# Query projection spread between the first attention steps, compressed-key softmax in two halves, six low parts on GpSimd

## The chip, the cores and the metric

The kernel runs on one core of a Trainium2 chip, in one launch. The metric is the device time of that launch in microseconds. Its engines are TensorE (PE; its weight loads are shown as PEld), VectorE (DVE), ScalarE (ACT), GpSimd (POOL) and the DMA queue of SyncE (SP). Each engine works through its own list of instructions in order and waits where an instruction needs what another engine has not yet delivered.

## The reference, cut to what matters

A two-layer decoder trunk for 256 tokens of width 1024, in float32: a retention layer with a dense SwiGLU, then a sparse-attention layer (16 heads in 4 groups) with a mixture of 8 experts. The change lies in the attention layer:

```python
proj = x @ w_q                                   # queries and gates
q = rotary(q, pos) * dh ** -0.5
gates = sigmoid(proj[..., H * dh:])              # three per head
sc = einsum('bgrqd,bgnd->bgrqn', qb, k_c)        # 15 compressed keys
p_cmp = masked_softmax(sc, cmp_end <= t)
o_cmp = einsum('bgrqn,bgnd->bgrqd', p_cmp, v_c)
...                                              # selected blocks, window
out = gb[..., 0:1] * o_cmp + gb[..., 1:2] * o_slc + gb[..., 2:3] * o_win
return out @ w_out
```

With 256 tokens every block is selected and the window holds all earlier tokens, so the second and the third branch are causal softmaxes over two sets of 256 keys (index `b` below).

## The kernel before

A list of steps is written out by hand (`step(units, fn)`), and the loop at the end of the program issues them in that order; the order of each engine's instructions follows from it. A unit is a piece of a weight matrix. It is loaded into a `raw` buffer by SP, and `convert` splits it into a high part (`whi`, a cast on ACT, L214) and a low part (`wlo`, the difference, on DVE, L215), so that a product takes three fast matmuls: high by high, low by high, high by low (L222 to L224). The loop converts up to `LOOK` = 3 units ahead of the step that uses them; a raw buffer is loaded again once both parts of its units are made. There are six `whi` and six `wlo` buffers.

The query projection has four groups `i` of 256 columns, with four units each (`b`, two of the eight rows of blocks of the contraction). `q_gemm(i, us, b)` does 12 matmuls for a unit, into two `acc` banks that are held until `b` = 3; then `rope` (four DVE instructions, L678 and L679, and two POOL additions, L684) makes `qn`, and `q_transpose(i)` turns it into two of the eight head pairs of `qT`.

Attention goes by head pairs `p` and token halves `t`. `att_scores(p, t)` multiplies queries and keys into two `mm` banks and adds the mask (L867, L870), takes the negative row maxima on DVE (L877, `anm`) and the exponentials with their sums on ACT (L879, `ae`, `asm`). `att_scale` turns the sums into weights (three small DVE instructions, L885 to L887) and scales the exponentials (L890, four instructions). `att_transpose` transposes them on PE and copies them out (`aPT`), and `att_values(p)` adds the compressed branch and the two others into one bank and splits it into `oh` and `ol`, a cast on ACT (L227) and a difference on DVE (L228).

`oh` and `ol` are made by `new_xT()` at `p` = 0. It allocates the same single pair of buffers, with the tags `xTh` and `xTl`, that holds the transposed input which the query projection reads.

The compressed branch has its own softmax for all 16 heads at once: `cmp_scores`, `cmp_weights`, `cmp_transpose`. After attention, `nsa_out` multiplies by the output weights (eight units of 128x1024, `nsa_o`), two layer norms follow, and the experts start. PSUM has four `mm` banks and four `acc` banks.

Of the kernel before, what the change touches and what calls it, by code (L numbers as in the profile page):

```python
# [10 lines left out]
F32 = mybir.dt.float32  # L11
F32R = mybir.dt.float32r
# [3 lines left out]
ALU = mybir.AluOpType  # L16
# [3 lines left out]
S = 256  # L20
NT = 2
# [5 lines left out]
NCMP = 15  # L27
# [57 lines left out]
class Unit:  # L85
    def __init__(self, raw, view, conv=True):
        self.raw = raw
        self.view = view
        self.conv = conv
        self.hi = self.lo = None  # L90
        self.own = False
        raw.left += 1


@with_exitstack
def tile_decoder(ctx, tc, x, ret_w_in, ret_gn_g, ret_w_out, nsa_w_kv, cmp_k_pe, cmp_k_w1, cmp_k_w2,
                 cmp_v_pe, cmp_v_w1, cmp_v_w2, nsa_w_q, nsa_w_out, ffn_w_in, ffn_w_out,
                 moe_router, moe_w_in, moe_w_out, ln_g, ln_b, tab_c, tab_r, out, wst, stop=None, cap=CAP):
    nc = tc.nc
# [8 lines left out]
    ident = sb.tile([128, 128], F32, name="ident")  # L108
# [96 lines left out]
    def convert(u, hi=None, lo=None):  # L205
        if not u.conv or u.hi is not None:
            return
        v = u.view(u.raw.ap)
        a, b = v.shape[1], v.shape[2]
        u.own = hi is not None  # L210
        u.hi = hi if u.own else side["pool"].tile([128, 1024], F32R, name="whi", tag="whi", bufs=NHL)
        u.lo = lo if u.own else side["pool"].tile([128, 1024], F32R, name="wlo", tag="wlo", bufs=NHL)
        u.hi, u.lo = (z[:, :a * b].rearrange("p (a b) -> p a b", a=a) for z in (u.hi, u.lo))
        nc.scalar.copy(u.hi, v)  # L214
        nc.vector.tensor_sub(u.lo, v, u.hi.bitcast(F32))  # L215
        release(u.raw)

    def step(units, fn, look=None):
        steps.append((units, fn, LOOK if look is None else look))
# [6 lines left out]
    def split(hi, lo, src):  # L226
        nc.scalar.copy(hi, src)  # L227
        nc.vector.tensor_sub(lo, src, hi.bitcast(F32))  # L228
# [135 lines left out]
    tsl = [slice(t * 128, (t + 1) * 128) for t in range(NT)]  # L364
# [4 lines left out]
    def open_phase(name):  # L369
        guard = tc.tile_pool(name=name, bufs=1, reuse_waits="tile")  # L370
        phases.append((guard, guard.__enter__()))
# [4 lines left out]
    def ptile(shape, dt, tag, bufs=1, lv=-1):  # L376
        return phases[lv][1].tile(shape, dt, name=tag, tag=tag, bufs=bufs)
# [285 lines left out]
    if stop not in ("r1", "r2"):  # L663
# [150 lines left out]
        def q_transpose(i):  # L814
            def f():
                ps = bank("acc")
                for t in range(NT):
                    for c in range(2):
                        nc.tensor.transpose(ps[:, c * 256 + t * 128:c * 256 + (t + 1) * 128],
                                            N["qn", i, t][:, 2 * c:2 * c + 2].rearrange("p h d -> p (h d)"), ident)  # L820
                nc.scalar.copy(N["qT"][:, 2 * i:2 * i + 2], ps.rearrange("p (c n) -> p c n", c=2))
            return f

        def cmp_scores():
            ps = bank("acc")
            for t in range(NT):
                for p in range(8):
                    nc.tensor.matmul(ps[:, (t * 8 + p) * 30:(t * 8 + p + 1) * 30], N["qT"][:, p, tsl[t]],
                                     N["kc"][:, p // 2].rearrange("p a n -> p (a n)"),
                                     start=t == 0 and p == 0, stop=True, skip_group_check=True)  # L830
            sc = ptile([128, NT, 16, NCMP], F32, "sc")
            shp = [128, NT, 16, NCMP]
            m = C[:, 264:294].rearrange("p (t n) -> p t n", t=2)[:, :, None, :].to_broadcast(shp)
            nc.vector.tensor_add(sc, ps[:, :480].rearrange("p (t h n) -> p t h n", t=2, h=16), m)
            mx = ptile([128, NT, 16], F32, "cmx")
            nc.vector.tensor_reduce(mx, sc, axis=AX.X, op=ALU.max)
            nc.vector.tensor_scalar(mx, mx, -1e29, None, op0=ALU.max)
            nc.vector.tensor_sub(sc, sc, mx[:, :, :, None].to_broadcast(shp))
            nc.scalar.activation(sc, sc, AF.Exp)
            N["ex"] = sc  # L840

        def cmp_weights():
            ex = N["ex"]
            sm = ptile([128, NT, 16], F32, "csm")
            nc.vector.tensor_reduce(sm, ex, axis=AX.X, op=ALU.add)
            nc.vector.tensor_scalar(sm, sm, 1e-30, None, op0=ALU.max)
            nc.vector.reciprocal(sm, sm)
            nc.vector.tensor_mul(sm, sm, N["gt"][:, :, :, 0])
            nc.vector.tensor_mul(ex, ex, sm[:, :, :, None].to_broadcast([128, NT, 16, NCMP]))

        def cmp_transpose():
            ps = bank("acc")
            for hb in range(2):
                for t in range(NT):
                    nc.tensor.transpose(ps[0:120, hb * 256 + t * 128:hb * 256 + (t + 1) * 128],
                                        N["ex"][:, t, hb * 8:hb * 8 + 8].rearrange("p h n -> p (h n)"), ident)
            hi, lo = ptile([120, 2, S], F32R, "pch"), ptile([120, 2, S], F32R, "pcl")
            split(hi, lo, ps[0:120].rearrange("p (b n) -> p b n", b=2))
            N["pcT"] = hi, lo

        def att_scores(p, t):

            g, n = p // 2, (t + 1) * 256
            ps = [bank() for _ in range(2)]
            for i in range(2):
                kt = N["kT"][i * 64:(i + 1) * 64, g].rearrange("p c b k -> p (c b k)")
                nc.tensor.matmul(ps[i][:, :n], N["qT"][i * 64:(i + 1) * 64, p, tsl[t]], kt[:, :n],  # L867
                                 start=True, stop=False, skip_group_check=True)
            for i in range(2):
                nc.tensor.matmul(ps[i][:, n - 256:n], identb, maskb.rearrange("p b k -> p (b k)"),  # L870
                                 start=False, stop=True, skip_group_check=True)
            e = ptile([128, 2, 2, t + 1, 128], F32, "ae%d" % t, bufs=2)
            sm = ptile([128, 2, 2], F32, "asm", bufs=6)
            nm = ptile([128, 2, 2], F32, "anm", bufs=6)
            for i in range(2):
                v = ps[i][:, :n].rearrange("p (c b k) -> p b c k", b=2, k=128)
                nc.vector.tensor_reduce(nm[:, i], v, axis=AX.XY, op=ALU.max, negate=True)  # L877
                for b in range(2):
                    nc.scalar.activation(e[:, i, b], v[:, b], AF.Exp, bias=nm[:, i, b:b + 1],  # L879
                                         accum_out=sm[:, i, b:b + 1])  # L880
            N["e", p, t] = e, sm

        def att_scale(p, t):
            e, sm = N["e", p, t]
            nc.vector.tensor_scalar(sm, sm, 1e-30, None, op0=ALU.max)  # L885
            nc.vector.reciprocal(sm, sm)
            nc.vector.tensor_mul(sm, sm, N["gt"][:, t, 2 * p:2 * p + 2, 1:3])  # L887
            for i in range(2):
                for b in range(2):
                    nc.vector.tensor_scalar(e[:, i, b], e[:, i, b], sm[:, i, b:b + 1], None, op0=ALU.mult)  # L890
# [88 lines left out]
        step([], lambda: kv_transpose(2))  # L979
        uqs = [units_q((wst['q0'], wst['q1']), i) for i in range(4)]  # L980

        def q_step(i):
            for b in range(4):
                step([uqs[i][b]], q_gemm(i, uqs[i], b))
                if i and b == 1:
                    step([], q_transpose(i - 1))

        q_step(0)
        step([], compress_out)
        step([], close_phase)  # L990
        step([], lambda: open_phase("nsa2"))
        for i in range(1, 4):
            q_step(i)
        step([], lambda: att_scores(0, 0))
        step([], lambda: att_scores(0, 1))
        step([], q_transpose(3))
        step([], lambda: att_scale(0, 0))
        step([], lambda: att_scale(0, 1))
        un = units_o(wst['nsa_o'], 0, 8)
        for p in range(7):  # L1000
            step([], lambda p=p: att_scores(p + 1, 0))
            step([], lambda p=p: att_transpose(p, 0))
            if p == 0:
                step([], cmp_scores)
            if p == 1:
                step([], cmp_transpose)
            step([], lambda p=p: att_scores(p + 1, 1))
            step([], lambda p=p: att_transpose(p, 1))
            step([], lambda p=p: att_scale(p + 1, 0))
            if p == 0:  # L1010
                step([], cmp_weights)
            else:
                step([], lambda p=p: att_values(p - 1))
            step([], lambda p=p: att_scale(p + 1, 1))
        nsa_out([0], un[0:1])
# [573 lines left out]
```

## Time and profile before

| what | value |
|---|---|
| time, median of 3 runs | 1461.58 us (1460.39 to 1463.45) |
| the profiled execution: its own time, and its span | 1460.46 us, 1458.7 us |
| PE matmul busy | 1355.4 us (93% of the span) |
| DVE, ACT, POOL busy | 471.3, 347.0, 62.7 us |
| query projection and attention, output projection | about 455 to 569 us of the span |
| experts | from about 589 us on |

The span runs from the first to the last instruction; the program's own time is 1.8 us longer. Busy shares are averages over stages with different limits, so the stage of the change is read by itself, from the timelines of single engines.

### The profile page before, as it was taken

Reading aid. Unit: us, or ns where it says so; the run is one execution under the profiler, and the core shown is the slowest. Engines: PE = TensorE matmul, PEld = TensorE weight load, DVE = VectorE, ACT = ScalarE, POOL = GpSimd, SP = SyncE. Lnnn points to the kernel's source line nnn. Section 1 sums busy time; section 2 is a strip of 40 time slices with the busy share of each in tenths; the row PEclk is TensorE's granted clock in tenths of the full one; section 3 lists DMA queues with packets and bytes.
Section 4 is the critical chain, followed back from the end, with each engine's and each line's share of the span. In section 5 each row is a group of like instructions: output and inputs, shape, how many; then the busy total and the mean of one; then the engine's idle time right before and its main releaser. Section 6 shows DMA issues by size and latency. Waiting matters only on the chain. (4 is left out here: it accounts for less than half of the span.)

```text
span 1458.7 us, 25366 instructions
## 1 busy us (share of the span) xinstructions
PE 1355.4 (93%) x11073; PEld 755.2 (52%) x11073; DVE 471.3 (32%) x845; ACT 347.0 (24%) x653; POOL 62.7 (4%) x74
## 2 busy tenths in 40 slices
PE   8999999999999988998999988888999988889995
PEld 7888888999978657432334332232333342222341
DVE  5755875554674886100100201001101101001002
ACT  4433434434534562200101110011001010000002
POOL 3101101000011000100000000000000000000000
PEclk9999999999999898999999999999999999999997
DMA  9736444544615308599999999999999999999970
GB/s 388 271 139 220 158 168 176 201 180 173 250 59 209 124 1 319 209 418 419 419 419 418 412 418 419 419 418 419 419 416 416 419 419 419 419 418 419 418 306 32
DMA packets 64022, 450.78 MB, mean 309 GB/s; under 512 B 7233, under 2 KB 7393, under 8 KB 10641
## 3 DMA queue, kind: packets, MB, share of 16 engines
q1 hardware_dynamic: 62208, 443.77, 75.4%
q0 software_dynamic: 1536, 4.98, 1.0%
q8 instruction: 106, 1.74, 0.5%
q14 instruction: 28, 0.22, 0.0%
q10 hardware_dynamic: 144, 0.07, 0.0%
HBM read 447.74 MB, written 1.05 MB: 308 GB/s over the span
## 5 line engine op out<-in xcount | busy, mean ns | idle before, releaser
L1202 PE MATMUL mm<-raw,xg 128*32 128x512 f32 (+1 forms) x2416 | 242.9, 544 | 11.5 <-DMA raw<-w_moe_a_dram 11.4
L1224 DVE TENSOR_TENSOR msh<-msh,mm 128x256 f32<-128x256 f32 (+1 forms) x96 | 35.5, 387 | 509.3 <-ACT msh L1223 509.3
L215 DVE TENSOR_TENSOR wlo<-raw,whi 128x1024 fp32r<-128x1024 f32 (+2 forms) x162 | 187.6, 1208 | 32.1 <-ACT whi L214 31.8
L1202 PE MATMUL mm<-ext,xg 128*32 128x512 f32 (+1 forms) x1808 | 178.8, 538 | 14.5 <-DMA ext<-w_moe_a_dram 14.5
L1202 PEld LDWEIGHTS mm<-raw,xg 128*32 128x32 f32 x2416 | 74.5, 110 | 164.4 <-issue 119.1
L214 ACT CAST whi<-raw 128x1024 fp32r<-128x1024 f32 (+2 forms) x162 | 153.7, 1008 | 18.6 <-PE acc L224 12.2
L1223 ACT ACTIVATE msh<-mm 128x256 f32<-128x256 f32 (+1 forms) x96 | 32.4, 357 | 492.9 <-PE mm L1202 492.9
L348 PE MATMUL mm<-xTh,whi 128*128 128x256 f32 x448 | 126.5, 282 | 1.6 <-ACT whi L214 1.6
L350 PE MATMUL mm<-xTh,wlo 128*128 128x256 f32 x448 | 125.9, 281 | 0.5 <-DVE wlo L215 0.5
L1261 PE MATMUL acc<-raw,hT 128*32 128x512 f32 x1000 | 116.5, 594 | 10.4 <-DMA raw<-w_moe_o_dram 9.2
L349 PE MATMUL mm<-xTl,whi 128*128 128x256 f32 x448 | 125.7, 281 | 0.0
L1202 PEld LDWEIGHTS mm<-ext,xg 128*32 128x32 f32 x1808 | 55.2, 110 | 129.3 <-issue 77.8
L1261 PE MATMUL acc<-ext,hT 128*32 128x512 f32 x864 | 98.4, 594 | 8.7 <-DMA ext<-w_moe_o_dram 8.7
L348 PEld LDWEIGHTS mm<-xTh,whi 128*128 128x128 f32 x448 | 84.7, 189 | 3.1 <-ACT whi L214 2.0
L350 PEld LDWEIGHTS mm<-xTh,wlo 128*128 128x128 f32 x448 | 84.7, 189 | 0.8 <-DVE wlo L215 0.8
L349 PEld LDWEIGHTS mm<-xTl,whi 128*128 128x128 f32 x448 | 84.7, 189 | 0.8
L1246 DVE COPY hT<-mm 128x256 f32<-128x256 f32 (+1 forms) x32 | 12.4, 389 | 223.2 <-PE mm L1239 223.2
L1261 PEld LDWEIGHTS acc<-raw,hT 128*32 128x32 f32 x1000 | 31.9, 110 | 87.9 <-issue 61.5
L1244 ACT COPY hT<-acc 128x512 f32<-128x512 f32 (+1 forms) x32 | 17.1, 536 | 230.6 <-PE acc L1239 150.1
L1202 PE MATMUL mm<-more,xg 128*32 128x512 f32 (+1 forms) x640 | 65.1, 535 | 4.9 <-DMA more<-w_moe_a_dram 4.8
L1261 PEld LDWEIGHTS acc<-ext,hT 128*32 128x32 f32 x864 | 26.4, 110 | 76.1 <-issue 50.8
L222 PE MATMUL mm<-whi,xTh 128*128 128x512 f32 (+1 forms) x144 | 55.6, 386 | 0.2 <-ACT xTh L227 0.2
(325 smaller groups left out, 1676.4 us busy)
## 6 DMA issues: line engine op xcount, KB each, us to landing
raw<-w_moe_a_dram SPq DMA_DIRECT2D x113, 1024.0 KB, 19.9
ext<-w_moe_a_dram SPq DMA_DIRECT2D x82, 1024.0 KB, 19.9
raw<-w_moe_o_dram SPq DMA_DIRECT2D x55, 1024.0 KB, 19.9
ext<-w_moe_o_dram SPq DMA_DIRECT2D x44, 1024.0 KB, 19.9
more<-w_moe_a_dram SPq DMA_DIRECT2D x29, 1024.0 KB, 19.9
raw<-w_ffn_b_dram SPq DMA_DIRECT2D x22, 1024.0 KB, 5.0
raw<-w_ret_a_dram SPq DMA_DIRECT2D x16, 1024.0 KB, 8.9
more<-w_moe_o_dram SPq DMA_DIRECT2D x13, 1024.0 KB, 19.9
```

The lines of the kernel that those rows point to most:

```text
L214: nc.scalar.copy(u.hi, v)
L215: nc.vector.tensor_sub(u.lo, v, u.hi.bitcast(F32))
L222: nc.tensor.matmul(ps, xh, wh, start=start, stop=False, skip_group_check=True)
L348: nc.tensor.matmul(ps, u.hi[:, k], xh[:, k], start=start and k == 0, stop=False, skip_group_check=True)
L349: nc.tensor.matmul(ps, u.hi[:, k], xl[:, k], start=False, stop=False, skip_group_check=True)
L350: nc.tensor.matmul(ps, u.lo[:, k], xh[:, k], start=False, stop=k == KD - 1, skip_group_check=True)
L1202: nc.tensor.matmul(M["A", g][j * 32:(j + 1) * 32, :n], M["xg", e // 2][:, k, e % 2, g * 32:(g + 1) * 32], v[:, kk, j], start=k == 0, stop= ...
L1223: nc.scalar.activation(sh[:, g, :w], M["A", g][:, :w], AF.Silu)
L1224: nc.vector.tensor_mul(sh[:, g, :w], sh[:, g, :w], M["A", g][:, w:2 * w])
L1244: nc.scalar.copy(dst, src)
L1246: nc.vector.tensor_copy(dst, src)
L1261: nc.tensor.matmul(M["y", g][q:q + 32], hT[0][:, g, cc, j * 32:(j + 1) * 32], v[:, c, h], start=s == 0 and i == 0, stop=s == 3 and i == 1, ...
```

## The change

The four units of the query groups 2 and 3 no longer come ahead of the attention steps but one by one behind `att_scores`: two in the opening (scores of pair 0), two in each of the turns `p` = 0, 1, 2. The compressed softmax is done for heads 0 to 7 at `p` = 0, 1 and for heads 8 to 15 at `p` = 3, 4. The sums of both token halves of a pair lie in one tile, and the three small instructions run once for a pair, in `att_scale(p, 0)`, instead of twice. The low parts of the first six output units are made by GpSimd instead of VectorE.

```diff
-        nc.vector.tensor_sub(u.lo, v, u.hi.bitcast(F32))
+        (nc.gpsimd if u.pool else nc.vector).tensor_sub(u.lo, v, u.hi.bitcast(F32))
...
-        def cmp_scores():
+        def cmp_scores(hb):
+
             ps = bank("acc")
             for t in range(NT):
-                for p in range(8):
-                    nc.tensor.matmul(ps[:, (t * 8 + p) * 30:(t * 8 + p + 1) * 30], N["qT"][:, p, tsl[t]],
+                for q in range(4):
+                    p = 4 * hb + q
+                    nc.tensor.matmul(ps[:, (t * 4 + q) * 30:(t * 4 + q + 1) * 30], N["qT"][:, p, tsl[t]],
                                      N["kc"][:, p // 2].rearrange("p a n -> p (a n)"),
...
-            sm = ptile([128, 2, 2], F32, "asm", bufs=6)
+            if t == 0:
+                N["asm", p] = ptile([128, NT, 2, 2], F32, "asm", bufs=4)
+            sm = N["asm", p][:, t]
...
-            nc.vector.tensor_scalar(sm, sm, 1e-30, None, op0=ALU.max)
-            nc.vector.reciprocal(sm, sm)
-            nc.vector.tensor_mul(sm, sm, N["gt"][:, t, 2 * p:2 * p + 2, 1:3])
+            if t == 0:
+                a = N["asm", p]
+                nc.vector.tensor_scalar(a, a, 1e-30, None, op0=ALU.max)
+                nc.vector.reciprocal(a, a)
+                nc.vector.tensor_mul(a, a, N["gt"][:, :, 2 * p:2 * p + 2, 1:3])
...
+        un = units_o(wst['nsa_o'], 0, 8)
+        for u in un[:6]:
+            u.pool = True
         step([], lambda: att_scores(0, 0))
+        q_unit(2, 0)
         step([], lambda: att_scores(0, 1))
+        q_unit(2, 1)
+        step([], q_transpose(1))
         step([], lambda: att_scale(0, 0))
         step([], lambda: att_scale(0, 1))
-        un = units_o(wst['nsa_o'], 0, 8)
+        more = {0: [(2, 2), (2, 3)], 1: [(3, 0), (3, 1)], 2: [(3, 2), (3, 3)]}
         for p in range(7):
             step([], lambda p=p: att_scores(p + 1, 0))
+            if p in more:
+                q_unit(*more[p][0])
             step([], lambda p=p: att_transpose(p, 0))
-            if p == 0:
-                step([], cmp_scores)
-            if p == 1:
-                step([], cmp_transpose)
+            if p in (0, 3):
+                step([], lambda p=p: cmp_scores(p // 3))
+            if p in (1, 4):
+                step([], lambda p=p: cmp_transpose(p // 3))
             step([], lambda p=p: att_scores(p + 1, 1))
+            if p in more:
+                q_unit(*more[p][1])
             step([], lambda p=p: att_transpose(p, 1))
+            if p in (1, 2):
+                step([], q_transpose(p + 1))
             step([], lambda p=p: att_scale(p + 1, 0))
-            if p == 0:
-                step([], cmp_weights)
-            else:
+            if p in (0, 3):
+                step([], lambda p=p: cmp_weights(p // 3))
+            if p:
                 step([], lambda p=p: att_values(p - 1))
```

In the changed kernel the lines named here are 1 to 17 higher: L215 is L216, L227 is L228, L877 is L881, L879 is L883, L684 is L685.

On VectorE, at the opening of attention, the maxima of the scores of pair 0 and of pair 1 stand close together before:

```order
L877 TENSOR_REDUCE anm<-mm 128x2 x4
L885 TENSOR_SCALAR asm<-asm 128x4
L886 RECIPROCAL asm<-asm 128x4
L887 TENSOR_TENSOR asm<-asm,gt 128x4
L890 TENSOR_SCALAR ae_4566<-ae_4566,asm 128x128 x4
```

In the changed kernel a low part of a query unit stands behind each pair of maxima:

```order
L881 TENSOR_REDUCE anm<-mm 128x2 x2
L216 TENSOR_TENSOR wlo<-raw,whi 128x512
L881 TENSOR_REDUCE anm<-mm 128x2 x2
L216 TENSOR_TENSOR wlo<-raw,whi 128x512
L891 TENSOR_SCALAR asm<-asm 128x8
L892 RECIPROCAL asm<-asm 128x8
L893 TENSOR_TENSOR asm<-asm,gt 128x8
L896 TENSOR_SCALAR ae_4390<-ae_4390,asm 128x128 x4
```

What moved: on ACT the high part (`whi`) of each such unit stands behind the exponentials of the same scores, and the low part here needs it.

On TensorE, around the first `att_values` (bank `acc_4697`) of the changed kernel, with buffer numbers (`xTh_3765` is the transposed input; `oh` is `xTh_4709` in the same memory):

```order
L933 MATMUL acc_4697<-aPT_4499,vn_3889 64x128 x2
L869 MATMUL mm_4717<-kT_3888,qT_4246 128x256
...
L223 MATMUL acc_4614<-whi_4536,xTh_3765 128x256
...
L906 MATMUL acc_4751<-ident_63,ae0_4599 128x128 x4
L869 MATMUL mm_4757<-kT_3888,qT_4246 128x512
...
L223 MATMUL acc_4614<-whi_4608,xTh_3765 128x256
L224 MATMUL acc_4614<-wlo_4609,xTh_3765 128x256
...
L820 MATMUL acc_4811<-ident_63,qn_4787 128x128 x2
```

What moved: the last two units of the projection, which read `xTh_3765`, now stand behind the first `att_values`, whose result is to be written to `xTh_4709`; before, all of them stood ahead of attention.

On GpSimd, the same stretch of the changed kernel (before, the eight `qn` additions followed each other with nothing but a memset between them):

```order
L685 TENSOR_TENSOR qn_4552<-t1k_4553,t1k_4554 128x256
L685 TENSOR_TENSOR qn_4558<-t1k_4559,t1k_4560 128x256
L216 TENSOR_TENSOR wlo_4657<-raw_4161,whi_4656 128x1024
L216 TENSOR_TENSOR wlo_4733<-raw_4161,whi_4732 128x1024
L216 TENSOR_TENSOR wlo_4772<-raw_4179,whi_4771 128x1024
L685 TENSOR_TENSOR qn_4787<-t1k_4788,t1k_4789 128x256
L685 TENSOR_TENSOR qn_4793<-t1k_4794,t1k_4795 128x256
```

What moved: three low parts of output units stand ahead of the additions that finish query group 3 (`qn_4787`, `qn_4793`), which PE's `q_transpose(3)` waits for.

## Rows read from the trace of the kernel before

**Rows 1.** Busy time by stretch: length, engines, granted clock, DMA share, GB/s.
```profile
468.65:544.85 76.20, 69.06 (x460) 47.35 (x459) 62.14 (x190) 45.73 (x165) 5.17 (x6) 0.93 0.22 83
...
498.00:506.00 8.00, 6.94 (x31) 4.61 (x33) 5.63 (x16) 3.69 (x15) 0.00 (x0) 0.57 0.00 0
...
544.85:569.04 24.19, 24.19 (x131) 19.14 (x130) 13.46 (x19) 7.25 (x10) 1.11 (x2) 1.00 0.68 261
...
589.00:603.00 14.00, 13.97 (x134) 4.12 (x126) 0.55 (x2) 2.25 (x5) 0.00 (x0) 1.00 0.01 2
...
700.00:1300.00 600.00, 552.49 (x5351) 195.02 (x5347) 64.08 (x144) 54.11 (x131) 5.94 (x12) 1.00 1.01 418
```
**Rows 2.** DVE timeline (start, length, instruction): opening and the turns' maxima.
```profile
470.71 2.01 DVE L215 TENSOR_TENSOR wlo<-raw,whi 128x512 fp32r<-128x512 f32 x2
...
483.98 1.94 DVE L877 TENSOR_REDUCE anm<-mm 128x2 f32<-128x256 f32 x4
...
489.46 0.75 DVE L877 TENSOR_REDUCE anm<-mm 128x2 f32<-128x256 f32 x2
...
500.50 0.75 DVE L877 TENSOR_REDUCE anm<-mm 128x2 f32<-128x256 f32 x2
...
509.50 1.94 DVE L877 TENSOR_REDUCE anm<-mm 128x2 f32<-128x256 f32 x4
...
516.61 1.94 DVE L877 TENSOR_REDUCE anm<-mm 128x2 f32<-128x256 f32 x4
```
**Rows 3.** ACT timeline: table load, exponentials, copies, casts.
```profile
479.29 2.00 ACT L214 CAST whi<-raw 128x1024 fp32r<-128x1024 f32 x2
481.31 1.28 ACT L879 ACT_TABLE_LOAD   x1
...
489.91 0.37 ACT L879 ACTIVATE ae<-mm,anm 128x128 f32<-128x128 f32 x1 [1.68 <-DVE anm L877]
...
491.30 0.60 ACT L901 COPY aPT<-acc 128x512 f32<-128x512 f32 x1
...
494.27 0.47 ACT L879 ACTIVATE ae<-mm,anm 128x256 f32<-128x256 f32 x1
...
496.09 0.60 ACT L912 COPY aPT<-acc 128x512 f32<-128x512 f32 x1
```
**Rows 4.** DVE timeline: low parts, compressed scores, one steady turn.
```profile
466.74 2.73 DVE L215 TENSOR_TENSOR wlo<-raw,whi 128x512 fp32r<-128x512 f32 x4
...
491.38 0.66 DVE L834 TENSOR_TENSOR sc<-acc,C 128x480 f32<-128x480 f32 x1 [1.17 <-PE acc L828]
...
512.55 0.87 DVE L890 TENSOR_SCALAR ae<-ae,asm 128x128 f32<-128x128 f32 x4
514.61 0.42 DVE L228 TENSOR_TENSOR xTl<-acc,xTh 128x256 fp32r<-128x256 f32 x1 [1.18 <-ACT xTh L227]
...
515.56 1.14 DVE L890 TENSOR_SCALAR ae<-ae,asm 128x256 f32<-128x256 f32 x4
```
**Rows 5.** PE timeline: two query units, then one steady turn.
```profile
478.52 0.37 PE L222 MATMUL acc<-whi,xTh 128*128 128x256 f32 x1
...
481.44 0.70 PE L867 MATMUL mm<-kT,qT 64*128 64x256 f32 x4
...
516.96 0.36 PE L222 MATMUL acc<-pch,vbh 120*128 120x256 f32 x1
...
518.94 0.70 PE L867 MATMUL mm<-kT,qT 64*128 64x256 f32 x4
...
520.86 1.20 PE L867 MATMUL mm<-kT,qT 64*128 64x512 f32 x4
```
**Rows 6.** POOL, timeline, then groups by form (busy us, mean ns, idle).
```profile
483.57 1.41 POOL L684 TENSOR_TENSOR qn<-t1k 128x256 f32<-128x256 f32 x2 [5.71 <-DVE t1k L679]
...
L408 POOL TENSOR_TENSOR rok<-t4k 128x256 f32<-128x256 f32 x4 | 6.9, 1716 | 0.0
...
L287 POOL TENSOR_TENSOR ygb<-msh,raw 128x512 f32<-128x512 f32 x2 | 2.5, 1268 | 183.1 <-ACT msh L286 183.1
```

More of the change, by code (lines that the diff above doesn't have):

```diff
@@ L91, in __init__ @@
         self.own = False
+        self.pool = False
         raw.left += 1
@@ L822, in q_transpose @@
             return f
-        def cmp_scores():
+        def cmp_scores(hb):
             ps = bank("acc")
             for t in range(NT):
-                for p in range(8):
-                    nc.tensor.matmul(ps[:, (t * 8 + p) * 30:(t * 8 + p + 1) * 30], N["qT"][:, p, tsl[t]],
+                for q in range(4):
+                    p = 4 * hb + q
+                    nc.tensor.matmul(ps[:, (t * 4 + q) * 30:(t * 4 + q + 1) * 30], N["qT"][:, p, tsl[t]],
                                      N["kc"][:, p // 2].rearrange("p a n -> p (a n)"),
-                                     start=t == 0 and p == 0, stop=True, skip_group_check=True)
-            sc = ptile([128, NT, 16, NCMP], F32, "sc")
-            shp = [128, NT, 16, NCMP]
+                                     start=t == 0 and q == 0, stop=True, skip_group_check=True)
+            shp = [128, NT, 8, NCMP]
+            sc = ptile(shp, F32, "sc", bufs=2)
             m = C[:, 264:294].rearrange("p (t n) -> p t n", t=2)[:, :, None, :].to_broadcast(shp)
-            nc.vector.tensor_add(sc, ps[:, :480].rearrange("p (t h n) -> p t h n", t=2, h=16), m)
-            mx = ptile([128, NT, 16], F32, "cmx")
+            nc.vector.tensor_add(sc, ps[:, :240].rearrange("p (t h n) -> p t h n", t=2, h=8), m)
+            mx = ptile([128, NT, 8], F32, "cmx", bufs=2)
             nc.vector.tensor_reduce(mx, sc, axis=AX.X, op=ALU.max)
@@ L839, in cmp_scores, with cmp_weights @@
             nc.scalar.activation(sc, sc, AF.Exp)
[L840 to L844, printed above, removed]
+            N["ex", hb] = sc
+        def cmp_weights(hb):
+            ex = N["ex", hb]
+            sm = ptile([128, NT, 8], F32, "csm", bufs=2)
             nc.vector.tensor_reduce(sm, ex, axis=AX.X, op=ALU.add)
@@ L847, in cmp_weights, with cmp_transpose @@
             nc.vector.reciprocal(sm, sm)
-            nc.vector.tensor_mul(sm, sm, N["gt"][:, :, :, 0])
-            nc.vector.tensor_mul(ex, ex, sm[:, :, :, None].to_broadcast([128, NT, 16, NCMP]))
-        def cmp_transpose():
+            nc.vector.tensor_mul(sm, sm, N["gt"][:, :, hb * 8:(hb + 1) * 8, 0])
+            nc.vector.tensor_mul(ex, ex, sm[:, :, :, None].to_broadcast([128, NT, 8, NCMP]))
+        def cmp_transpose(hb):
             ps = bank("acc")
[L853 to L859, printed above, removed]
+            for t in range(NT):
+                nc.tensor.transpose(ps[0:120, tsl[t]], N["ex", hb][:, t].rearrange("p h n -> p (h n)"), ident)
+            if hb == 0:
+                N["pcT"] = ptile([120, 2, S], F32R, "pch"), ptile([120, 2, S], F32R, "pcl")
+            hi, lo = N["pcT"]
+            split(hi[:, hb], lo[:, hb], ps[0:120, 0:256])
         def att_scores(p, t):
@@ L980, in tile_decoder, with q_unit @@
         uqs = [units_q((wst['q0'], wst['q1']), i) for i in range(4)]
-        def q_step(i):
+        def q_unit(i, b):
+            step([uqs[i][b]], q_gemm(i, uqs[i], b))
+        for i in range(2):
             for b in range(4):
-                step([uqs[i][b]], q_gemm(i, uqs[i], b))
+                q_unit(i, b)
                 if i and b == 1:
                     step([], q_transpose(i - 1))
[L988 to L993, printed above, removed]
+            if i == 0:
+                step([], compress_out)
+                step([], close_phase)
+                step([], lambda: open_phase("nsa2"))
+        un = units_o(wst['nsa_o'], 0, 8)
+        for u in un[:6]:
+            u.pool = True
         step([], lambda: att_scores(0, 0))
+        q_unit(2, 0)
         step([], lambda: att_scores(0, 1))
-        step([], q_transpose(3))
+        q_unit(2, 1)
+        step([], q_transpose(1))
         step([], lambda: att_scale(0, 0))
         step([], lambda: att_scale(0, 1))
-        un = units_o(wst['nsa_o'], 0, 8)
+        more = {0: [(2, 2), (2, 3)], 1: [(3, 0), (3, 1)], 2: [(3, 2), (3, 3)]}
         for p in range(7):
             step([], lambda p=p: att_scores(p + 1, 0))
+            if p in more:
+                q_unit(*more[p][0])
             step([], lambda p=p: att_transpose(p, 0))
-            if p == 0:
-                step([], cmp_scores)
-            if p == 1:
-                step([], cmp_transpose)
+            if p in (0, 3):
+                step([], lambda p=p: cmp_scores(p // 3))
+            if p in (1, 4):
+                step([], lambda p=p: cmp_transpose(p // 3))
             step([], lambda p=p: att_scores(p + 1, 1))
+            if p in more:
+                q_unit(*more[p][1])
             step([], lambda p=p: att_transpose(p, 1))
+            if p in (1, 2):
+                step([], q_transpose(p + 1))
             step([], lambda p=p: att_scale(p + 1, 0))
-            if p == 0:
-                step([], cmp_weights)
-            else:
+            if p in (0, 3):
+                step([], lambda p=p: cmp_weights(p // 3))
+            if p:
                 step([], lambda p=p: att_values(p - 1))
```

## The prediction

> **What bounds the kernel now.** Read the busy times by stretch first [rows 1]. From 700 to 1300 us the transfers run at 418 GB/s and a DMA share of 1.01, so the experts are paced by their weights. Just ahead of that, from 589 to 603 us, next to nothing is moved (2 GB/s): every buffer is full and SP waits until the first expert frees one. The whole rest therefore starts when attention and output projection are done, and a microsecond gained or lost there comes out one for one at the end. The output projection (544.85 to 569.04) has PE busy for 24.19 of 24.19 us, so what DVE and POOL do there lies under PE. Query group 2 to the end of attention, 468.65 to 544.85, takes 76.20 us with PE busy for 69.06 and DVE for 62.14: neither is full, the stretch is a chain between engines.
>
> The second view is DVE's timeline [rows 2]. Each turn of the attention loop begins with the row maxima. The rope of query group 1 ends at 470.71, where the next instruction starts; the first maxima come at 483.98, then 489.46, 500.50, 509.50 and 516.61, and from there a turn takes 7.1. So the first three turns take 5.5, 11.0 and 9.0 us; the second and third hold the whole compressed softmax, and part of them ran with PE at 1.2 GHz (0.57 of the clock granted from 498 to 506 [rows 1]).
>
> A turn is a chain DVE, ACT, DVE: maxima, exponentials of both halves on ACT, then on DVE the scaling, then the next maxima. The prices on it: 0.45 from the start of the maxima to the first exponential (489.46 to 489.91), 1.39 for the four exponentials of half 0 and 1.82 for those of half 1, 0.6 for a copy, 1.0 for a cast of 1024 columns, so about 0.5 for 512 [rows 3]. For half 1 I take 0.7 to the first exponential (an estimate, between 0.45 and twice that). On DVE: 0.68 for a low part of 512 columns (2.73 for four), 0.87 and 1.14 for the scalings, 0.95 from `xTl` to the end of the three small instructions, that is 0.35 and 0.6 [rows 4].
>
> **What the change takes away.** Eight query units leave the front of attention. In the new order the maxima of pair 0 stand right behind the group-1 rope, so they can start at 470.71 instead of 483.98: **13.3 us earlier**. Half of the small trios go (8 x 0.6 = 4.8 us of DVE), but the trio now also needs the exponentials of half 1. In a steady turn DVE today waits for the cast of `oh`, which stands on ACT behind those exponentials (1.18 [rows 4]); in the new order the trio and the first scaling wait there instead. I cost this at nothing; without that cover it is 0.6 a turn either way. The six low parts that leave DVE free nothing on the path, since PE is full in the output projection; if that cover were gone, each would cost some 1.2 more there (2 x 1.268 on POOL, as in the last group of rows, against at most 2 x 0.68).
>
> **What it adds, turn by turn.** A unit's high part stands on ACT behind the exponentials, its low part on DVE ahead of the next maxima or scaling, so all of it falls into the chain.
>
> Turn 0 to 1: 0.45, the table load 1.28 (hidden before, it ended at 482.59 while ACT still waited [rows 3]), 1.39, cast 0.5, low part 0.68, 0.7, 1.82, cast 0.5, low part 0.68, trio 0.6, scalings 0.87 and 1.14. Together 10.6 against 5.5: **+5.1**.
>
> Turn 1 to 2: the same without the table load (9.3), with half of the compressed maxima block and half of its weights (each about 1.3: three instructions of 240 columns near 0.37, estimated between 0.66 for 480 and 0.42 for 256 columns [rows 4], and small ones), the rope of group 2 (1.4, four of 256 columns) and a copy 0.6. Together 13.9 against 11.0: **+2.9**.
>
> Turn 2 to 3: 0.45, 1.39, cast 0.5, copy 0.6, the compressed cast and difference 0.7, 0.7, 1.82, cast of an output unit 1.0, copy 0.6: 7.8 until PE can start `att_values(0)`. Its result goes to `oh`, which lies in the memory of the transposed input, and the last readers of that are the units (3, 2) and (3, 3), behind it on PE. So ACT's cast waits for values 1.98 (516.96 to 518.94), scores and transposes of half 0 1.92 (to 520.86), a query unit 1.46 (two in 2.92, 478.52 to 481.44), scores of half 1 1.6 (1.20 and the masks), a second unit 1.46 [rows 5]: 8.4. Behind that cast on ACT stand all exponentials of pair 3; behind DVE's difference stands the scaling that PE's transposes need. With cast 0.4, difference 0.35 and scaling 1.14 the turn is 18.1 against 9.0: **+9.1**, 6.4 of it the wait for the old buffer.
>
> Turn 3 to 4: `q_transpose(3)` stands ahead of `att_values(1)` on PE and needs `qn` of group 3, which on POOL stands behind three low parts; the last of these needs the third output cast, behind the exponentials of pair 3. So: 0.45, 1.39, cast 1.0, copy 0.6, 1.82, cast 1.0, low part 2.5 (2 x 1.268), two additions 1.4 (1.41 for two) [rows 6], transposes 0.4, values 1.98, cast 0.4, difference 0.35, scaling 1.14. Together 14.4 against 7.1: **+7.3**.
>
> Turn 4 to 5 takes in the second half of the compressed maxima and weights, **+2.6**; turn 5 to 6 their cast and difference between the two exponentials, **+0.7**. The rest is as before.
>
> The turns grow by 27.7 and the start gains 13.3: **+14.4**. Two prices are open. PE idles for some 5 us in turn 3 to 4; if it falls to 1.2 GHz as from 498 to 506, values, scores and transposes behind that double: nothing to +4. A low part on POOL costs 2.5 from the 1268 ns row, but 6.9 at the `rok` row's 1716 ns for 256 columns; DVE mostly waits while the one that counts runs, so the lower row is the nearer. I take 1.5 for both: +15.9. On the profiled execution's 1460.46 us (span 1458.7 and 1.8 around it) that is 1476.4; the median of the runs is 1.1 above that execution, so **1477**.
>
> The Trainium skill (SBUF — State Buffer, Who interferes with whom) says that a VectorE instruction with two SBUF inputs and a GpSimd instruction that reads SBUF exclude each other, the second waiting for the whole first. The rows agree: 1716 ns for `rok`, which runs beside DVE's low parts, against 0.70 us for `qn` of the same size [rows 6]. By it a low part on POOL would wait for up to one DVE instruction, about 1.0 each, and the sum would be 1478 instead of 1477.
>
> **Rivals.** *PE fills its gaps (faster).* The units take PE's idle 7.1 us (76.20 less 69.06), DVE has 8.4 us less to do (the trios and three low parts of about 1.2 that lie in this stretch), and the stretch shrinks to PE's work: 1454. For it: DVE's 62.14 is far below the span. It decides when the turns grow by less than 13.3 instead of 27.7, that is, if neither long wait exists and the units cost about 1.5 each in the chain. Against it: both waits follow from the order of in-order engines. Chance 0.07.
>
> *The two effects cancel (no change).* The turns grow by about 13: 1459 to 1464, which needs one of the long waits gone and the first turns half as long. 0.05.
>
> *One long wait is mostly covered.* If ACT reaches the `oh` cast late, or POOL makes its low parts early, 4 to 10 us go: 1467 to 1473. For it: in a steady turn that cast stands 4 us behind the maxima anyway. 0.14.
>
> *POOL at the `rok` price.* One low part of 6.9 in turn 3 to 4 is +4.4, and the clock may add up to 4: 1480 to 1486. For it: `rok` is the same operation beside the same DVE work. 0.12.
>
> *The forecast,* 1472 to 1481: 0.62.
>
> **How the numbers follow.** About 0.2% (2.9 us) is what a measurement of this kernel can tell from no change. Slower by more than that are the forecast, the covered wait and the dear POOL: 0.88. Same 0.05, faster 0.07. The range 1465 to 1485 leaves out the first two rivals and a little of the last, under 0.2.
>
> **What would show it.** First maxima about 13 us earlier; the turns then some 10.6, 13.9, 18.1 and 14.4 us long; a wait of ACT at the first cast of `oh` of about 6 us, ended by a PE matmul of the query projection; a wait of PE at `q_transpose` for POOL's `qn` of several us; the table load between the first maxima and the first exponential; GpSimd low parts near 2.5; the expert stage as long as before. I am wrong if the turns stay near 7 to 11 us, which would mean that the high and low parts are made beside the exponentials and not between them, or if the expert stage changes its length.

## The result, and the profile of the changed kernel

The changed kernel takes 1481.93 us (median of 4 runs, 1481.40 to 1483.16) against 1462.16: ratio 1.0131, 95% interval [1.0109, 1.0153], 19.8 us slower. The forecast was 1477 us, and slower. Its profiled execution took 1482.43 us with a span of 1480.5. Ratios are compared below, not medians: executions of one kernel differ by up to 9 us with the stretches in which PE runs at half speed (in two profiles of the changed kernel its granted clock from 465 to 470 us was 1.00 and 0.75, and the first maxima came at 471.27 and 472.96; in that of `own_buffer` it was 0.50, and they came at 474.24).

DVE's timeline of the changed kernel, the maxima that begin a turn, answers to [rows 2]:

```profile
471.27 0.75 DVE L881 TENSOR_REDUCE anm<-mm 128x2 f32<-128x256 f32 x2
482.05 0.74 DVE L881 TENSOR_REDUCE anm<-mm 128x2 f32<-128x256 f32 x2
496.50 0.75 DVE L881 TENSOR_REDUCE anm<-mm 128x2 f32<-128x256 f32 x2
513.58 1.94 DVE L881 TENSOR_REDUCE anm<-mm 128x2 f32<-128x256 f32 x4
529.38 0.74 DVE L881 TENSOR_REDUCE anm<-mm 128x2 f32<-128x256 f32 x2
539.05 0.75 DVE L881 TENSOR_REDUCE anm<-mm 128x2 f32<-128x256 f32 x2
547.64 1.94 DVE L881 TENSOR_REDUCE anm<-mm 128x2 f32<-128x256 f32 x4
554.75 1.34 DVE L881 TENSOR_REDUCE anm<-mm 128x2 f32<-128x256 f32 x3
```

The first maxima come 12.7 us earlier (483.98 in [rows 2]). The turns then take 10.8, 14.5, 17.1, 15.8, 9.7, 8.6 and 7.1 us; before they took 5.5, 11.0, 9.0 and four times 7.1. That is 29.7 us more. From the timelines of single engines, the rows that make the two longest turns, and one behind them:

```profile
471.75 1.28 ACT L883 ACT_TABLE_LOAD   x1 [2.53 <-issue]
...
503.42 3.02 DVE L896 TENSOR_SCALAR ae<-ae,asm 128x128 f32<-128x128 f32 x4
...
511.79 0.37 ACT L228 CAST xTh<-acc 128x256 fp32r<-128x256 f32 x1 [7.13 <-PE acc L224]
512.19 0.42 DVE L229 TENSOR_TENSOR xTl<-acc,xTh 128x256 fp32r<-128x256 f32 x1 [5.75 <-ACT xTh L228]
...
518.64 1.09 ACT L215 CAST whi<-raw 128x1024 fp32r<-128x1024 f32 x1
519.80 2.40 POOL L216 TENSOR_TENSOR wlo<-raw,whi 128x1024 fp32r<-128x1024 f32 x1 [0.91 <-DVE ae L896]
522.18 1.40 POOL L685 TENSOR_TENSOR qn<-t1k 128x256 f32<-128x256 f32 x2
522.95 1.37 PE L820 MATMUL acc<-ident,qn 128*128 128x128 f32 x4 [5.99 <-POOL qn L685]
523.97 0.56 PE L223 MATMUL acc<-pch,vbh 120*128 120x256 f32 x1
...
524.89 2.65 PE L933 MATMUL acc<-aPT,vn 128*64 128x256 f32 x16
...
560.83 3.32 DVE L896 TENSOR_SCALAR ae<-ae,asm 128x256 f32<-128x256 f32 x4
...
587.18 1.41 DVE L290 SCALAR_TENSOR_TENSOR X<-msh,rs,ygb 128x512 f32<-128x512 f32 x2 [2.39 <-DMA ygb<-in_ln_b_dram]
```

Read it from top to bottom. The table load stands between the first maxima and the first exponential. ACT stands for 7.13 us at the first cast of the attention output, until PE has done the last query unit; DVE waits behind it. In the next turn the third output cast, the low part on GpSimd (its row names DVE; the cast that it needs ended at 519.73) and the two additions lead to PE's transposes, which waited 5.99 us. In the last row the layer norm waits for its own weights. In the windows PE's clock stands in the third column from the end (full speed is 1.00, 2.4 GHz):

```profile
513.58:520.00 6.42, 0.70 (x5) 0.42 (x4) 4.93 (x16) 5.97 (x20) 2.54 (x2) 0.76 0.10 11
520.00:529.38 9.38, 6.43 (x40) 4.54 (x40) 4.37 (x7) 1.17 (x3) 3.58 (x3) 0.62 0.26 106
529.38:560.00 30.62, 25.66 (x184) 16.59 (x184) 22.29 (x72) 19.38 (x79) 0.00 (x0) 1.00 0.00 1
```

PE was busy for 0.70 of 6.42 us, and transposes and values then ran largely at 1.2 GHz.

### The profile page after: what moved, and what is told of

The parts are those of the page before. It is cut to its first block, busy times and chain, and to the rows that moved or that the text cites. A ratio compares the mean times of both kernels' runs of the same rounds, so it can differ in the third digit from the quotient of the medians.

```text
span 1480.5 us, 25334 instructions
## 1 busy us (share of the span) xinstructions
PE 1355.6 (92%) x11073; PEld 753.5 (51%) x11073; DVE 469.6 (32%) x825; ACT 347.7 (23%) x655; POOL 76.1 (5%) x80
## 5 line engine op out<-in xcount | busy, mean ns | idle before, releaser
L1219 PE MATMUL mm<-ext,xg 128*32 128x512 f32 (+1 forms) x1808 | 179.4, 538 | 15.8 <-DMA ext<-w_moe_a_dram 15.6
L216 DVE TENSOR_TENSOR wlo<-raw,whi 128x1024 fp32r<-128x1024 f32 (+2 forms) x156 | 180.8, 1208 | 40.7 <-ACT whi L215 40.5
L215 ACT CAST whi<-raw 128x1024 fp32r<-128x1024 f32 (+2 forms) x162 | 154.4, 1009 | 18.9 <-PE acc L225 12.2
L1278 PE MATMUL acc<-raw,hT 128*32 128x512 f32 x1000 | 116.0, 594 | 10.4 <-DMA raw<-w_moe_o_dram 9.4
L1278 PEld LDWEIGHTS acc<-raw,hT 128*32 128x32 f32 x1000 | 31.4, 110 | 88.0 <-issue 60.1
L1261 ACT COPY hT<-acc 128x512 f32<-128x512 f32 (+1 forms) x32 | 17.1, 535 | 229.8 <-PE acc L1256 149.6
```

Of the source, the lines that this page charges most:

```text
L216: (nc.gpsimd if u.pool else nc.vector).tensor_sub(u.lo, v, u.hi.bitcast(F32))
L1219: nc.tensor.matmul(M["A", g][j * 32:(j + 1) * 32, :n], M["xg", e // 2][:, k, e % 2, g * 32:(g + 1) * 32], v[:, kk, j], start=k == 0, stop= ...
L1261: nc.scalar.copy(dst, src)
L1278: nc.tensor.matmul(M["y", g][q:q + 32], hT[0][:, g, cc, j * 32:(j + 1) * 32], v[:, c, h], start=s == 0 and i == 0, stop=s == 3 and i == 1, ...
```

## The experiments

All ratios are to the kernel before. Two ratios whose intervals overlap widely are not told apart: two half-widths of 0.25% leave about 0.35% (5 us) of doubt in a difference. "Turns" are from the profiled execution; "norm" is the time from the first row maxima of the last pair to the end of the second layer norm.

| kernel | ratio, 95% | first maxima | turns | norm |
|---|---|---|---|---|
| before | 1 | 483.98 | 5.5 11.0 9.0 7.1 7.1 7.1 7.1 | 36.5 |
| changed | 1.0131 [1.0109, 1.0153] | 471.27 | 10.8 14.5 17.1 15.8 9.7 8.6 7.1 | 39.5 |
| `after_again` | 1.0133 [1.0109, 1.0157] | 472.96 | 10.8 14.4 17.1 15.8 9.7 8.6 7.1 | 39.5 |
| `own_buffer` | 1.0092 [1.0065, 1.0118] | 474.24 | 10.8 15.2 13.2 16.0 10.0 8.6 7.1 | 38.9 |
| `late_split` | 1.0111 [1.0083, 1.0138] | 471.17 | 10.8 14.5 16.1 12.0 11.1 10.7 7.1 | 39.6 |
| `own_and_late` | 1.0092 [1.0065, 1.0119] | 471.08 | 10.8 14.5 10.7 12.0 11.1 10.8 7.1 | 40.2 |
| `own_late_early` | 1.0088 [1.0059, 1.0116] | 472.06 | 7.6 14.5 10.8 12.0 11.1 10.7 7.1 | 39.8 |
| `low_on_dve` | 1.0150 [1.0122, 1.0178] | 471.14 | 10.8 14.4 20.5 17.1 10.5 8.6 7.1 | 38.1 |
| `low_first3` | 1.0125 [1.0098, 1.0151] | 470.93 | 10.8 14.5 17.1 15.3 9.7 8.6 7.1 | 38.1 |
| `no_interleave` | 1.0034 [1.0013, 1.0055] | 485.73 | 6.6 12.8 8.6 7.1 10.4 8.6 7.1 | 39.6 |
| `halves_and_merge` | 1.0041 [1.0024, 1.0058] | 484.13 | 6.3 11.9 8.6 7.1 9.2 8.6 7.1 | 38.3 |
| `halves_alone` | 0.9995 [0.9978, 1.0012] | 487.06 | 5.5 10.5 8.6 7.1 8.7 8.5 7.1 | 36.9 |
| `group3_between` | 1.0024 [1.0011, 1.0037] | 476.44 | 5.7 9.2 13.0 9.3 10.6 10.9 7.1 | 36.5 |
| `group3_front` | 1.0014 [0.9998, 1.0030] | 481.81 | 5.5 9.4 12.7 7.6 8.7 8.5 9.2 | 38.2 |

**The changed kernel again**, to tie the chips together.

> The changed kernel itself once more, beside the next three on the same chip. Every theory expects the ratio measured first, 1.0131, within 0.002.

It came out so.

**`own_buffer`: the wait for the old buffer.**

> The changed kernel, but the output of head pair 0 goes into a buffer of its own (one of the six of the high parts) instead of the transposed input's memory. Theory (the wait for the old readers stands in the chain): ACT's 7.1 us wait at the first cast of the attention output goes, the turn from pair 2 to pair 3 falls from 17.1 us to about 11.5, the time falls by 5 to 6 us to about 1476. Rival (the same units on PE, or GpSimd's queue, are late next): the turn after it grows by what this one loses, and the time stays within 2 us of the changed kernel's 1482.

```diff
-                N["oh"], N["ol"] = new_xT()
-            split(N["oh"][:, p], N["ol"][:, p], po[:, 0:256])
+                o = side["pool"].tile([128, 1024], F32R, name="whi", tag="whi", bufs=NHL)
+                N["oc", 0] = o[:, 0:S], o[:, S:2 * S]
+            else:
+                if p == 1:
+                    N["oh"], N["ol"] = new_xT()
+                N["oc", p] = N["oh"][:, p], N["ol"][:, p]
+            split(*N["oc", p], po[:, 0:256])
...
```

0.4% less than the changed kernel, 6 us with some 5 us of doubt. Timeline of ACT and PE, and a window:

```profile
511.58 0.37 ACT L228 CAST whi<-acc 128x256 fp32r<-128x256 f32 x1 [3.27 <-PE acc L933]
...
522.74 1.37 PE L820 MATMUL acc<-ident,qn 128*128 128x128 f32 x4 [4.81 <-POOL qn L685]
```

```profile
508.00:512.00 4.00, 4.00 (x23) 2.55 (x23) 2.12 (x3) 0.69 (x2) 1.82 (x1) 0.60 0.00 0
```

The wait that is left (3.27) is for the values themselves, and the turn fell to 13.2, not to 11.5: here PE ran at a granted clock of 0.60 from 508 to 512 us (1.00 in the changed kernel), and the values took 3.6 us instead of 2.1. With the values at full speed, in `own_and_late` below, the same turn is 10.7. The next turn stayed at 16.0, so the second wait is a term of its own, against the rival, in which the next turn takes the gain back.

**`late_split`: GpSimd's queue ahead of `qn`.**

> The changed kernel, but the first three output units are split into high and low part in the turns from pair 3 on, one per turn, instead of in the turns with the query units, so that GpSimd makes query group 3 ahead of them. Theory (PE's 6.0 us wait for the query heads behind three low parts stands in the chain, and the casts of these units too): that wait goes, the turn from pair 3 to pair 4 falls from 15.8 us to 8 to 10, the time falls by 6 to 7 us to about 1475. Rival (the casts and low parts cost the same wherever they stand): the later turns grow by 1 to 2 us each and the time stays within 2 us of 1482.

```diff
+            if p in (3, 4, 5):
+                un[p - 3].gate = len(steps)
...
-        while state["conv"] < lim and sum(
+        while state["conv"] < lim and flat[state["conv"]].gate <= n and sum(
...
```

The ratio fell by 0.2%, well inside the intervals: no gain in time is shown, as the rival has it. PE's wait is gone and its turn fell by 3.8, as the theory has it, but only to 12.0 instead of 8 to 10, and the two turns behind it grew, by 1.4 and 2.1. The timeline shows one instruction held up in each of these three turns, which begin at 512.53, 524.51 and 535.61:

```profile
516.09 1.38 PE L821 MATMUL acc<-ident,qn 128*128 128x128 f32 x4
...
521.36 3.23 DVE L897 TENSOR_SCALAR ae<-ae,asm 128x256 f32<-128x256 f32 x4
522.01 2.43 POOL L217 TENSOR_TENSOR wlo<-raw,whi 128x1024 fp32r<-128x1024 f32 x1 [5.29 <-ACT whi L216]
...
531.00 2.34 POOL L217 TENSOR_TENSOR wlo<-raw,whi 128x1024 fp32r<-128x1024 f32 x1 [6.57 <-ACT whi L216]
531.13 2.24 DVE L850 TENSOR_SCALAR csm<-csm 128x16 f32<-128x16 f32 x1
...
543.15 3.25 DVE L897 TENSOR_SCALAR ae<-ae,asm 128x256 f32<-128x256 f32 x4
543.21 2.52 POOL L217 TENSOR_TENSOR wlo<-raw,whi 128x1024 fp32r<-128x1024 f32 x1 [9.87 <-ACT whi L216]
```

Four scalings of this size take 1.13 to 1.15 us otherwise, and the small instruction of the compressed weights 0.17; beside a low part on GpSimd they take about 2.1 us more. More on this at the end.

**`own_and_late`: both.**

> Both edits at once: the output of pair 0 in a buffer of its own, and the first three output units split from pair 3 on. Theory (the two waits are separate terms of the sum, and each edit alone moved part of its gain into the other wait): the gains add up to 9 to 11 us, ratio to the kernel before about 1.006, the turns from pair 2 on 11 to 13, 10 to 11, 10, 9 and 7 us. Rival (the casts of the output units fill the later turns whatever is done): no better than the own buffer alone, ratio 1.009.

The diffs are the two above. Turn 2 to 3 fell by 6.4 and turn 3 to 4 by 3.8, so in the turns the waits were separate terms; the later turns are 1 to 2 us longer than the theory has them, by the instructions held up as in `late_split`. The turns add up to 77.0 instead of 83.5, but the ratio is that of the own buffer alone, the rival's number, with 1.006 just outside the interval. A gain of both edits over one is not shown in the time; how much of it the interval hides stays open.

**`own_late_early`: splits in the chain.**

> As the one with both edits, and the look-ahead at the last query unit before attention is 6 instead of 3, so that six units are split before attention begins. Theory (high and low parts of a unit stand in the chain of a turn): the turn from pair 0 to pair 1 falls from 10.8 us to about 7.7, the first maxima come about 1 us later, the time falls by a further 1.5 to 2 us, ratio about 1.005. Rival (they lie beside the exponentials, and PE's units themselves make the turn long): the turn stays at 10 or more.

```diff
-            step([uqs[i][b]], q_gemm(i, uqs[i], b))
+            step([uqs[i][b]], q_gemm(i, uqs[i], b), look=6 if (i, b) == (1, 3) else None)
```

DVE's timeline of the first turn, which answers to the chain of the prediction:

```profile
472.06 2.05 DVE L882 TENSOR_REDUCE anm<-mm 128x2 f32<-128x256 f32 x4
477.20 0.17 DVE L892 TENSOR_SCALAR asm<-asm 128x8 f32<-128x8 f32 x1 [3.09 <-ACT ae L884]
...
479.70 0.75 DVE L882 TENSOR_REDUCE anm<-mm 128x2 f32<-128x256 f32 x2
```

7.6 us, as the theory has it, at a start 1.0 us later: the splits stood in the chain. The time did not fall by the 1.5 to 2 us that the theory has, though the second norm ended 2.6 us earlier than in `own_and_late` (585.65 against 588.25). The windows from there on and SP's first load of the next expert show where it went:

```profile
594.65:600.65 6.00, 6.00 (x29) 6.00 (x29) 0.00 (x0) 1.44 (x3) 5.38 (x1) 0.50 0.02 7
600.65:606.65 6.00, 6.00 (x38) 1.63 (x41) 0.00 (x0) 1.76 (x2) 0.00 (x0) 0.66 0.00 0
```

```profile
617.01 1.97 SPq L190 DMA_DIRECT2D raw<-w_moe_o_dram  x4
```

PE, never idle in them, ran at half speed far into the second window (the same two stretches behind the norm had 0.63 and 1.00 in `own_and_late`), and the loads began at 617.01, against 616.88 in `own_and_late`.

**`low_on_dve`: low parts back on VectorE.**

> The changed kernel with all low parts on VectorE, as before the change. Theory (GpSimd's queue alone makes the turn from pair 3 to pair 4 long): PE's wait for the query heads goes, the time falls by 4 to 6 us to about 1477. Rival (three low parts of 1.2 us come back into VectorE's part of the chain, between maxima and scalings, and take what the wait gave): the time stays or grows by up to 3 us, 1481 to 1485.

```diff
-        for u in un[:6]:
-            u.pool = True
```

No gain, as the rival has it; the ratio is 0.17% higher, inside the intervals. PE's wait did not even go, for DVE now made the rope late (timeline of POOL and PE):

```profile
526.64 1.41 POOL L685 TENSOR_TENSOR qn<-t1k 128x256 f32<-128x256 f32 x2 [34.07 <-DVE t1k L680]
527.42 1.37 PE L820 MATMUL acc<-ident,qn 128*128 128x128 f32 x4 [5.97 <-POOL qn L685]
```

DVE began the rope at 525.72, behind two low parts of 1.2 us in this turn and the maxima of both halves. The turn before it grew too, from 17.1 to 20.5; there PE's clock was 0.50 from 504 to 508 us, where the values run, against 1.00 in the changed kernel.

**`no_interleave`: everything but the moved units.**

> The changed kernel with all query units ahead of the attention loop again; the compressed softmax by halves, the merged small instructions and the low parts on GpSimd stay. Theory (the placement of the units and its two waits make the whole loss): the first maxima start near 484 us again, the first turns are 6 to 10 us long, the time is 1460 to 1464, like the kernel before. Rival (the second half of the compressed softmax, which costs 2.6 and 1.5 us in two later turns, is not given back in the early ones): 1465 to 1468.

```diff
-        for i in range(2):
+        for i in range(4):
...
-        more = {0: [(2, 2), (2, 3)], 1: [(3, 0), (3, 1)], 2: [(3, 2), (3, 3)]}
+        more = {}
...
```

0.34%: the rival's size, though not its cause. The moved units make 1.0133 less 1.0034, about 1.0% or 14 us (5 us of doubt); about 5 us come from the rest. The next two show which part.

**`halves_alone` and `halves_and_merge`.**

> The kernel before, with the compressed softmax by halves of the heads and nothing else of the change. Theory (the second half costs 2.6 and 1.5 us in two later turns, the early turns win back about 2): ratio 1.001 to 1.003. Rival A (all of the loss of the version without the moved units, ratio 1.0034, is the halves): 1.0034. Rival B (the halves cost nothing, the merged small instructions and GpSimd's low parts made that loss): within 1.0005 of 1.

> The kernel before with the compressed softmax by halves and the merged small instructions, all query units ahead, all low parts on VectorE. Theory (the merged instructions wait for the exponentials of half 1, so the first turn grows by about 1 us and the others not at all): ratio 1.000 to 1.001, which leaves 3 to 4 us of the loss of the version without the moved units to GpSimd's low parts. Rival (the merge makes that loss): 1.003.

The diffs are those of the change: `cmp_scores`, `cmp_weights`, `cmp_transpose` by halves of the heads in the first; the block `if t == 0` of the small instructions in `att_scale` too in the second. The halves cost nothing that can be measured (rival B of the first); the merge makes the loss, against the theory of the second. DVE's first turn of both, `halves_alone` first:

```profile
489.05 0.17 DVE L887 TENSOR_SCALAR asm<-asm 128x4 f32<-128x4 f32 x1
...
490.87 0.17 DVE L887 TENSOR_SCALAR asm<-asm 128x4 f32<-128x4 f32 x1 [0.33 <-ACT ae L881]
```

```profile
487.93 0.17 DVE L891 TENSOR_SCALAR asm<-asm 128x8 f32<-128x8 f32 x1 [1.86 <-ACT ae L883]
```

Merged, the trio and the scaling of half 0 wait for the exponentials of half 1 (1.86 against 0.33). The first two turns grow by 0.8 and 1.4, one later by 0.5, the stretch to the norm by 1.4; that is 4.1 of some 6.7 us, and the rest I have not placed.

**`low_first3`: the layer norm's wait.**

> The changed kernel with the low parts of output units 3 to 5, which lie under the output projection, on VectorE again; those of units 0 to 2 stay on GpSimd. Theory (these three low parts delay the load of the layer norm's second row, which then lands after VectorE wants it): the load lands in 9 to 10 us instead of 12.2, the wait of 2.4 us goes, 2 to 2.5 us faster than the changed kernel. Rival (the wait comes from the weight loads beside it, whatever makes the low parts): the wait stays, the same time.

```diff
-        for u in un[:6]:
+        for u in un[:3]:
```

The second row now lands 9.8 us after its issue, and the norm stands for 0.31 us at most where it stood for 2.39:

```profile
584.92 1.41 DVE L290 SCALAR_TENSOR_TENSOR X<-msh,rs,ygb 128x512 f32<-128x512 f32 x2 [0.31 <-DVE rs L283]
```

The stretch to the end of the norm fell by 1.4 us; the ratio moved by 0.08% (1.2 us), within its interval, so the 2 to 2.5 us are not shown. That GpSimd's low parts alone slow the load is not shown either: in `halves_and_merge`, which has none, it landed 10.7 us after its issue and VectorE waited 1.15 us. Why the load is slow was not tried.

**Two attempts to beat the kernel before.**

> A version that may beat the kernel before: only the four units of query group 3 between the first steps (two in each of the first two turns, so that all are read before the first output is written), six units split before attention, the first three output units split from pair 3 on with low parts on GpSimd, the small instructions per half as before the change. Theory (start earlier by 6.6 to 7.6 us; the turns grow by 0.5, -1.7, 2.2, 0, 2.1 and 1.5 us, 4 to 5 in all): 2 to 4 us faster than before, ratio 0.998. Rival (the turns grow as they did in the change, by 5 and 3 us in the first two): 1.003 or more.

> Another version that may beat the kernel before: the four units of query group 3 in the first two turns as in the earlier try, these four and the first two output units split before attention begins, so that none of their splitting lies in a turn; the third output unit in the last turn, with its low part on GpSimd; the other low parts on VectorE; transposes of group 3 one turn later; small instructions per half. Theory (splits in the turns are what made the earlier try 0.24% slower): turns near 5.6, 9.5, 11, 7.5, 9, 8.6 and 7.1 us, start 5 to 6 us earlier than before, ratio 0.997 to 0.999. Rival (the start is given back by the front, which now has the splits of six units): 1.001 or more.

```diff
-        for i in range(2):
+        for i in range(3):
...
-        more = {0: [(2, 2), (2, 3)], 1: [(3, 0), (3, 1)], 2: [(3, 2), (3, 3)]}
+        more = {0: [(3, 0), (3, 1)], 1: [(3, 2), (3, 3)]}
...
```

The first is slower: its start (7.5 us earlier) and its first two turns (5.7 and 9.2) are as expected, but the later ones grew by 4.0, 2.2, 3.5 and 3.9. In each of the last three a VectorE instruction is held up beside GpSimd: two scalings of 3.3 us, and one of the three small instructions with 2.02 us for 0.16. The second can't be told from the kernel before: its start is 2.2 us earlier instead of 5 to 6, which is its rival, and its last turn has such a scaling too. In turn 2 to 3 of both, 13.0 and 12.7 us long, PE came to the values at half speed (granted clock 0.57 from 498 to 502 us in the first, 0.50 from 502 to 506 in the second). No version was faster.

## Why the prediction was right, step by step

| step | predicted | profile |
|---|---|---|
| start | -13.3 | -12.7 |
| turns 0 to 1, 1 to 2 | +5.1, +2.9 | +5.3, +3.4 |
| turn 2 to 3 | +9.1 | +8.1 |
| turn 3 to 4 | +7.3 | +8.7 |
| turns 4 to 5, 5 to 6 | +2.6, +0.7 | +2.6, +1.5 |
| open prices, and behind the turns | +1.5 | +4.8 |
| sum | +15.9 | +21.8 |

The first four rows carry the result, and their terms are the measured ones within 1.4 us; the 4.8 us at the bottom arose behind the turns, where the prediction had put nothing, for its 1.5 of open prices belong to turn 3 to 4. Its median of 1477 is 4.9 us short, and 1481.93 lies just above its own band of 1472 to 1481.

**The chain.** That splits made between the exponentials lengthen a turn is shown by `own_late_early` (10.8 to 7.6). The two long waits are where the prediction put them; `own_buffer` and `late_split` take one each away and leave the other.

**The wait for the old buffer** was put at 6.4 us of the turn. Taken away, with `late_split` as the base, it gave 5.4 (16.1 to 10.7); from the changed kernel it gave 3.9, since the values then ran at half speed. **The wait for `qn`** stands, but not only for the reason given: without low parts on GpSimd it is as long, since DVE then makes the rope later.

**Mis-sized terms.** Turn 3 to 4 lacked the half clock: the transposes took 1.37 us for which I had 0.4, the values 3.57 (523.97 to 527.54) for which I had 1.98; against that, PE started after the first of the two additions, 0.6 earlier than I had it. "Nothing to +4" was the open price of this. "The rest is as before" was wrong by 4.8 us: 3.0 up to the end of the second norm, of them 2.4 the wait for `ygb` and 0.7 ahead of the first norm, then 1.0 until the loads begin (29.3 us after the norm instead of 28.3), and 0.8 behind that. I had the output projection cover everything that DVE and POOL do there, without looking at the load of the norm's weights behind it.

**"One for one at the end"** held only roughly: from the end of the second norm to the first load of the next expert it is 28.3 to 31.4 us in these profiles, so up to 3 us won or lost ahead of it can vanish or appear there.

**The merged trio** I took as free in a steady turn, rightly (7.1 stays); in the early turns, where no cast of the output covers it, it stands in the chain, and it makes the kernel 0.46% slower than the halves alone do.

**The rivals.** PE filling its gaps, and the two effects cancelling, are refuted: even with both waits away the ratio is 1.009. One long wait mostly covered is refuted by the rows: ACT waited 7.13 us and PE 5.99. GpSimd at the `rok` price is refuted as a price: its low parts took 2.35 to 2.45 us; it was VectorE that waited, as the last section shows. But the time came out in that rival's band, by the terms above.

## What to carry to other kernels

Work moved into a loop that is a chain between engines costs its length in the chain, not its length on the engine that has gaps: count the splits, the waits and the buffers' old readers, not the idle PE. A saving of a few small instructions that makes the first half wait for the second is a loss where nothing else covers that wait. An operation moved to GpSimd is not off VectorE's path if VectorE has a scaling to do meanwhile: here each low part in a late turn held one up by about 2 us. Taking a wait away pays less than its length where the work behind it, or the clock, takes part of it back.

## What the runs showed of the hardware

**GpSimd stops VectorE's scalings.** In every profile with low parts on GpSimd beside attention, a scaling that meets one takes up to 2.4 to 2.6 us instead of 0.3, and ends just behind it; the longest of 64 is 0.35 us before and in `low_on_dve` and `halves_and_merge`, which have none. The small instruction at 531.13 in `late_split` (128x16, 2.24 us for 0.17) ended with the low part too, at 533.37 against 533.34. In all traces together 28 such VectorE instructions take over 1.5 us, and each ends 0.03 to 0.15 us behind a low part on GpSimd. A low part on VectorE was held up too: at 570.18 in the changed kernel one took 2.63 us, where others take 1.23, beside one on GpSimd (569.28, 2.45 us). The operations of one line in three kernels, the changed one, `low_on_dve` and `halves_and_merge` (ns: least, median, most):

```profile
L896 DVE TENSOR_SCALAR ae<-ae,asm x64: 273/343/2534, 480.2 to 563.8; 128x128 f32<-128x128 f32 x32, 128x256 f32<-128x256 f32 x32
```

```profile
L896 DVE TENSOR_SCALAR ae<-ae,asm x64: 278/316/351, 480.1 to 567.1; 128x128 f32<-128x128 f32 x32, 128x256 f32<-128x256 f32 x32
```

```profile
L896 DVE TENSOR_SCALAR ae<-ae,asm x64: 279/318/352, 488.6 to 549.7; 128x128 f32<-128x128 f32 x32, 128x256 f32<-128x256 f32 x32
```

The Trainium skill (SBUF — State Buffer, Who interferes with whom) says that `tensor_scalar` can enter a two-port mode, and that whichever of VectorE and GpSimd comes first then blocks the other for its whole instruction; these rows agree. The prediction weighed this section of the Trainium skill only for instructions with two inputs, and only for GpSimd's waiting. In the changed kernel two of the three long groups of scalings (503.42, 519.47) lie under the two waits; in `late_split` and `group3_between` the held-up instructions stand in the chain, about 2.1 us each.

**The clock takes gains back.** PE runs at half speed when the dispatch to the experts begins, and returns to full speed at times that differ, though PE is busy without a gap in that stretch: from 9 to 15 us after the second norm the mean was 0.67 before, 0.51 in the changed kernel and 0.50 in `own_late_early`, and the loads began 28.3, 29.3 and 31.4 us after it. What decides that moment these runs do not show.
